# Mixing stage of a hybrid decoder trunk: both head pairs of the recurrence take its steps together, decay and key tiles first, placed by a clock

## The chip, the cores and the metric

The kernel runs on one core of one Trainium2 chip. The metric is device time in microseconds (us) of a whole execution, as the median of several runs. The profile is of one further execution, taken by the hardware profiler; TensorE is called PE in it, VectorE DVE, ScalarE ACT, GpSimd POOL and SyncE SP.

## The reference

Two layers, each a feed-forward half (SwiGLU), a mixing of tokens, and a second feed-forward half, over 512 tokens of width 1024. The change lies in the mixing, whose input projection gives 20 tiles of 128 columns: attention (8 query heads, 2 key/value heads, window 128), RWKV-7 (4 heads of 64) and a short gated convolution. Cut to what matters:

```python
def rwkv7_time_mix(p, mu, w0, w_w2, a0, a_w2, w_g2, k_k, k_a, r_k, gn_w, gn_b):
    p = p + mu * (token_shift(p) - p)
    r, k, v, wd, ad, gd = jnp.split(p, ...)
    w_log = -jax.nn.softplus(-(w0 + jnp.tanh(wd) @ w_w2)) - 0.5
    decay = jnp.exp(-jnp.exp(w_log))
    a = jax.nn.sigmoid(a0 + ad @ a_w2)
    g = jax.nn.sigmoid(gd) @ w_g2
    kk = (k * k_k) / norm over each head
    k = k * (1.0 + (a - 1.0) * k_a)
    def step(S, inp):                       # one token; S is 64x64 a head
        s_kk = S @ kk_t
        S = S * w_t - s_kk (kk_t * a_t) + v_t k_t
        return S, S @ r_t
    ...
    y = groupnorm(y) * gn_w + gn_b          # mean and variance of each head
    return (y + sum(r * k * r_k) * v) * g
```

## The kernel before

Everything is kept transposed: features on the 128 partitions, the 512 tokens along the row. The large projections are done in three products each (mm3, L117 to L123), on values split into a high part and a remainder: L121 high weights by high input, L122 high weights by the remainder, L123 the weights' remainder by the high input. Weights arrive whole (wraw, two buffers); ScalarE casts them to wH (L133) and VectorE subtracts to get wL (L135), four buffers each. A tile of 128 output columns is 8 x 3 products of 128x512, in PSUM under the tag "mm" (two banks). The recurrence of each head pair has a PSUM tag of its own (r0, r1), attention uses "x", two banks each.

The recurrence is worked in chunks of 64 tokens. A head pair q (two heads, 128 partitions) goes through rwkv(q), in this order, with PE's steps by the names that the trace shows:

- ps_w and ps_a (L753, L755): decay and rate from the low-rank tile lo. ps_kk: the norms of the keys. VectorE: cumulative products P of the decay (16 scans for both pairs, L771), their reciprocal iP (L779), the reciprocal norm rn (L780), kk, k and the scaled tiles.
- ps_bo: the bonus. ps_c (L811): two sets of chunk products, B and K.
- An inverse of each chunk's triangular matrix: 16x16 blocks go by DMA to a layout of 64 partitions, are inverted there in 15 double steps on VectorE (elim, L839), and come back by DMA. Two levels of products (ps_x, ps_t, ps_tt, L897) join the blocks.
- ps_vN, ps_beN, ps_kaN, ps_ta (L853): transposes. ps_xv (L874), ps_w (L916): their products with the inverse. The result, negated, is AX/Wn (L917).
- ps_gn (L926 to L930) and ps_o (L942 to L946): each chunk's transition and output. ps_s (L954): six sequential state steps. ps_ys (L960).
- ps_m, ps_v (headsum, L610), ps_g (L980): the group norm's mean and variance, and the gate.

Each of these products is between 64x64 blocks of the two heads and two chunk parities. A block stands on rows 0 to 63 or 64 to 127 of the array by the partitions of its input, and on its columns by the partitions of its output. ps_gn and ps_o use all four combinations of halves; ps_x, ps_t, ps_tt, ps_w (L916) and ps_xv use two, since the output keeps its input's half.

Attention goes through four blocks of 128 queries: scores (ps_sc, L1001, L1003), softmax on ScalarE (exponentials, L1026) and VectorE, transposes (ps_pt, L1041) and ps_av (L1059).

The order: products() is a generator that yields after each large product; it delivers the 20 tiles (keys kt and values of attention, queries 0 to 3, then lo, k0, r0, v0, k1, r1, v1, gd, six of the convolution), and then six tiles of the output projection, which need attention. rwkv(0), rwkv(1) and attention are generators too; each yields the PE time of the step just issued. A loop gives them credit in proportion to the work left:

```python
while credit > 0 and more:
    product_step()          # one group of large products, 0.65 of credit
```

with the work of a pair set to 29.8, attention 15.2 and the products 129.6. Each engine then runs its queue in order. In shape, small tiles before the activations (gap, gap2, shift, shift2) set where the tiles lie in the memory.

Of the kernel before, what the change touches and what calls it, by code (L numbers as in the profile page):

```python
# [17 lines left out]
P = 128  # L18
# [14 lines left out]
GAP = 448  # L33
GROUPS = ((0, 12), (12, 22))
RWKV_WORK, ATT_WORK, FILL_WORK = 29.8, 15.2, 129.6


def _columns(spec):
# [14 lines left out]
    ("ident", P), ("bones", P), ("bones2", 2), ("su", CH), ("iu", CH), ("diag", CH),  # L53
# [5 lines left out]
def trunk_kernel(ctx, tc, ins, out, layers=L, phases=("ffn1", "mix", "ffn2")):  # L59
# [7 lines left out]
    shift = ctx.enter_context(tc.tile_pool(name="shift", bufs=1))  # L67
    shift.tile([P, GAP // 4], F32, name="shift")
    hnp = [ctx.enter_context(tc.tile_pool(name=n, bufs=KD)) for n in ("hnp", "hnp2")]
    shift = ctx.enter_context(tc.tile_pool(name="shift2", bufs=1))  # L70
    shift.tile([P, (512 - GAP) // 4], F32, name="shift2")
# [45 lines left out]
    def mm3(acc, w, k, x, sl, start, stop):  # L117

        wH, wL, xH, xL = w[0][:, k], w[1][:, k], weave(x[0][:, sl]), weave(x[1][:, sl])
        acc = paired(acc)  # L120
        mm(acc, wH, xH, start=start, stop=False)  # L121
        mm(acc, wH, xL, start=False, stop=False)  # L122
        mm(acc, wL, xH, start=False, stop=stop)  # L123
# [213 lines left out]
    def ffn(l, w_in, w_pair, w_out, hn, im, ss, need, then, first, ready, coming):  # L337
# [6 lines left out]
        with tc.tile_pool(name="act", bufs=1) as ap_:  # L344
            ap_.tile([P, GAP // 4], F32, name="gap", tag="gap")
            com = {n: tuple(ap_.tile([P, 4, H2], F32R, name=x, tag="com", bufs=8) for x in ("comH", "comL")) for n in ("P1", "P2", "T3", "T4")}
            ap_.tile([P, (512 - GAP) // 4], F32, name="gap2", tag="gap2")
# [235 lines left out]
    def mix(l, hn, ss, mp, then, ready):  # L583
# [42 lines left out]
        def shifted(pt, j, z):  # L626

            act(pt.like(z), pt.view, AF.Copy, scale=got["om"][:, j : j + 1])
            for b, n in enumerate((T // 2, T // 2 - 1)):
                later = z[:, b * T // 2 + 1 :][:, :n]  # L630
                stt(later, pt.view[:, b, :n], mu[:, j : j + 1], later, ALU.mult, ALU.add)
            return z

        def products():
# [10 lines left out]


# [6 lines left out]
            got.update(om=om, w0h=w0h, a0h=a0h)  # L653
            kt = A("kt")
# [6 lines left out]
            yield  # L661
            pv = psum([P, NB, P], "ps_vt")
            for b in range(NB):
                nc.tensor.transpose(pv[:, b], vr[:, b * P : (b + 1) * P], cst("ident"))
# [4 lines left out]
            rq4 = rq.rearrange("p (b i g) -> p b i g", i=4, g=2)  # L669
            for i in range(4):  # L670
# [4 lines left out]
                if i == 1:  # L675
                    pk = headsum(ksq, "ps_ks")
# [4 lines left out]
                sq = EA("qsq")  # L681
                act(pt.like(sq), pt.view, AF.Square)
                yield
                pq = psum([P, NB, 2], "ps_q")
                for b in range(NB):
                    mm(pq[:, b], sq[:, b * P : (b + 1) * P], cst("bones2"), start=True, stop=True)
                act(rq4[:, :, i], pq, AF.Sqrt, bias=vals["eps64"])
            nc.vector.reciprocal(rq, rq)
# [3 lines left out]
            got["lo"] = shifted((yield from tile_()), 6, S(1, "lo"))  # L692
            act(got["lo"][:64], got["lo"][:64], AF.Tanh)
# [51 lines left out]
        def rwkv(q):  # L745

            R = f"r{q}"
            c1 = slice(q, q + 1)
            cw = slice(q * P, (q + 1) * P)
            lo = got["lo"]  # L750

            pw = psum([P, T], "ps_w", R)
            mm(pw, lw[:64, cw], lo[:64], start=True, stop=True)  # L753
            pa = psum([P, T], "ps_a", R)
            mm(pa, lw[64:, cw], lo[64:], start=True, stop=True)  # L755
            yield 1.7
            kp = prm(l, "kk")[:, c1]
            sq = EQ(q, "kksq")
            act(sq, k_[q], AF.Square, scale=kp)
            d0 = EQ(q, "decay")  # L760
            act(d0, pw, AF.Tanh, bias=got["w0h"][:, c1], scale=0.5)
            act(d0, d0, AF.Exp, bias=vals["nhb"], scale=-HB)
            a_ = S(q, "a")
            act(a_, pa, AF.Tanh, bias=got["a0h"][:, c1], scale=0.5)
            pk = headsum(sq, "ps_kk", R)
            yield 0.9
            ts(a_, a_, 0.5, 0.5, ALU.mult, ALU.add)
            Pt = S(q, "P")
            for c in range(NC):
                cs = slice(c * CH, (c + 1) * CH)  # L770
                nc.vector.tensor_tensor_scan(Pt[:, cs], d0[:, cs], zero, 1.0, ALU.mult, ALU.add)  # L771
            pc = small(f"pc{q}", NC)
            nc.vector.tensor_copy(pc, Pt[:, CH - 1 :: CH])

            rn = EQ(q, "rn")
            ts(rn, pk, 1e-24, None, ALU.max)
            act(rn, rn, AF.Sqrt)
            iP = S(q, "iP")
            nc.vector.reciprocal(iP, Pt)  # L779
            nc.vector.reciprocal(rn, rn)  # L780
            kk = S(q, "kk")
            stt(kk, k_[q], kp, rn, ALU.mult, ALU.mult)
            t = EQ(q, "k2")
            ts(t, a_, -1.0, prm(l, "ka")[:, c1], ALU.add, ALU.mult)
            k2 = k_[q]
            stt(k2, t, 1.0, k2, ALU.add, ALU.mult)
            bo = S(q, "bonus")
            stt(bo, r_[q], prm(l, "rk")[:, c1], k2, ALU.mult, ALU.mult)
            pb = headsum(bo, "ps_bo", R)
            yield 0.9  # L790

            AR = U(q, "AR", [P, 2, NC, CH])
            tt(AR[:, 0, :, 1:], chunks(Pt)[:, :, : CH - 1], chunks(kk)[:, :, 1:], ALU.mult)
            nc.vector.tensor_copy(AR[:, 0, :, 0], chunks(kk)[:, :, 0])
            be = a_
            tt(be, kk, a_, ALU.mult)
            tt(be, be, iP, ALU.mult)
            tt(AR[:, 1], chunks(r_[q]), chunks(Pt), ALU.mult)
            ka = iP
            tt(ka, k2, iP, ALU.mult)  # L800
            tt(bo, pb, v_[q], ALU.mult)


            def pairs(src, name):
                M = U(q, name, [P, 2, NB, 2, CH])
                pts = [psum([P, NB, 2, CH], "ps_c", R) for _ in range(2)]
                for b in range(NB):
                    for c in range(2):
                        n = 2 * b + c
                        for e in range(2):  # L810
                            mm(pts[e][rows[c], b], src[rows[e], n * CH : (n + 1) * CH], AR[rows[e], :, n], start=True, stop=True)  # L811
                msk = con[:, CON["su"][0] : CON["iu"][1]].unsqueeze(1).to_broadcast([P, NB, 2 * CH])
                for e in range(2):
                    tt(M[:, e].rearrange("p b a t -> p b (a t)"), pts[e].rearrange("p b a t -> p b (a t)"), msk, ALU.mult)
                yield 1.4
                return M

            B_ = yield from pairs(be, "B")
            LT = B_[:, :, :, 0]
# [551 lines left out]
```

## Time and profile before

| | |
|---|---|
| time, median of 3 runs | 1866.52 us (1865.02 to 1866.69) |
| the profiled execution | 1866.04 us, its span 1864.0 us |
| PE busy | 1828.7 us, 98% of the span |
| VectorE busy | 1398.4 us, 75% |
| ScalarE busy | 836.3 us, 45% |
| GpSimd busy | 130.9 us, 7% |
| DMA | 308.24 MB, mean 165 GB/s |
| mixing stage, layer 1 | 372.77 to 615.56 us |
| mixing stage, layer 2 | 1286.62 to 1529.21 us |

A page of the profile tells shares of the span; a group of instructions is given as line, engine, operation, output and inputs, shape, count, then busy time and mean duration in ns, then the engine's idle time just before and what ended it. In a timeline each row is start, duration, engine, line and instruction. Matmuls overlap their successors, so a row's duration is longer than the distance to the next.

### The profile page before, as it was taken

The page shows a single profiled execution, that of the slowest core. Times are in us where ns is not written, and L with a number is a line of the kernel's source. Part 1 is how long each engine was busy: PE and PEld are TensorE (multiplying, and loading weights), DVE is VectorE, ACT ScalarE, POOL GpSimd, SP SyncE. Part 2 cuts the span into 40 slices and gives each one's busy share as a digit, 9 for nine tenths or more (in the row PEclk, how much of TensorE's full clock was granted, in tenths as well). Part 3 has the DMA queues.
Part 4 walks back from the last instruction along what each step waited for, and adds up shares of the span by engine and source line. Part 5 has one row for each costly group of instructions (what it writes and reads, how often), then busy time and mean ns, then how long its engine had stood idle before and what let it go on. Part 6 is the DMA issues. An engine that isn't in the chain of part 4 may idle for free.

```text
span 1864.0 us, 33421 instructions
## 1 busy us (share of the span) xinstructions
PE 1828.7 (98%) x13664; PEld 1644.4 (88%) x13664; DVE 1398.4 (75%) x2202; ACT 836.3 (45%) x1272; POOL 130.9 (7%) x212
## 2 busy tenths in 40 slices
PE   8999999999999999999999999999999999999999
PEld 6889899986777999899999988999767788998998
DVE  7687677867986887777878786777589778874872
ACT  4443255346422555245345524544563335532551
POOL 0101110100000000110100020110000000100100
PEclk8999999999999999999999999999999999999999
DMA  7667876621122475886737688773212125775752
GB/s 307 225 185 234 263 197 202 221 83 46 58 55 72 136 195 176 296 223 195 246 112 197 171 272 228 192 229 114 101 56 59 53 68 161 209 227 139 203 144 68
DMA packets 104313, 308.24 MB, mean 165 GB/s; under 512 B 23392, under 2 KB 24416, under 8 KB 103136
## 3 DMA queue, kind: packets, MB, share of 16 engines
q1 hardware_dynamic: 75936, 203.34, 32.3%
q0 software_dynamic: 28224, 102.77, 21.7%
q8 instruction: 107, 1.75, 0.4%
q14 instruction: 46, 0.38, 0.1%
HBM read 302.66 MB, written 3.41 MB: 164 GB/s over the span
## 4 chain that ended last, share of the span: by engine, by line
PE 71%; DVE 13%; DMA 7%; issue 4%; ACT 4%; POOL 1%; SPq 0%; POOLq 0%; DVEq 0%; ACTq 0%
PE ps_mm L121 11%; PE ps_mm L122 10%; PE ps_mm L123 10%; PE ps_d L420 6%; PE ps_d L422 6%; PE ps_d L421 6%; PE ps_f L420 3%; PE ps_f L422 3%; PE ps_f L421 3%; DMA wada<-in_wadaT 2%; DVE wL L135 2%; PE ps_g L422 2%; PE ps_g L420 2%; PE ps_g L421 2%; ACT wH L133 1%
## 5 line engine op out<-in xcount | busy, mean ns | idle before, releaser
L133 ACT CAST wH<-wraw 128x1024 fp32r<-128x1024 f32 (+2 forms) x292 | 266.1, 918 | 434.7 <-PE ps_mm L122 190.2
L135 DVE TENSOR_TENSOR wL<-wraw,wH 128x1024 fp32r<-128x1024 f32 (+2 forms) x292 | 307.2, 1058 | 105.1 <-ACT wH L133 104.4
L123 PE MATMUL ps_mm<-actH,wL 128*128 128x512 f32 (+1 forms) x784 | 281.5, 359 | 2.8 <-DVE wL L135 2.8
L121 PE MATMUL ps_mm<-actH,wH 128*128 128x512 f32 (+1 forms) x784 | 281.6, 359 | 0.0
L122 PE MATMUL ps_mm<-actL,wH 128*128 128x512 f32 (+1 forms) x784 | 281.2, 359 | 0.0
L121 PE MATMUL ps_mm<-hnH,wH 128*128 128x512 f32 (+1 forms) x760 | 267.5, 359 | 5.7 <-ACT hnH L133 2.9
L122 PE MATMUL ps_mm<-hnL,wH 128*128 128x512 f32 (+1 forms) x760 | 266.5, 353 | 0.5
L123 PE MATMUL ps_mm<-hnH,wL 128*128 128x512 f32 (+1 forms) x760 | 266.4, 353 | 0.6 <-DVE wL L135 0.6
L420 PE MATMUL ps_d<-comH,wH 128*128 128x256 f32 x816 | 224.7, 275 | 0.3 <-ACT s L446 0.3
L421 PE MATMUL ps_d<-comL,wH 128*128 128x256 f32 x816 | 224.4, 275 | 0.0
L422 PE MATMUL ps_d<-comH,wL 128*128 128x256 f32 x816 | 224.4, 275 | 0.0
L192 DVE SCALAR_TENSOR_TENSOR wada<-wada,crep 128x1024 f32<-128x1024 f32 x140 | 167.7, 1219 | 48.8 <-DMA wada<-in_wadaT 48.2
L135 DVE TENSOR_TENSOR wL<-sum,wH 128x1024 fp32r<-128x1024 f32 x102 | 124.9, 1224 | 71.5 <-ACT wH L133 71.3
L123 PEld LDWEIGHTS ps_mm<-actH,wL 128*128 128x128 f32 x784 | 149.1, 190 | 20.3 <-DVE wL L135 3.6
L121 PEld LDWEIGHTS ps_mm<-hnH,wH 128*128 128x128 f32 x760 | 143.4, 191 | 24.9 <-issue 3.8
L121 PEld LDWEIGHTS ps_mm<-actH,wH 128*128 128x128 f32 x784 | 149.1, 190 | 16.8
L122 PEld LDWEIGHTS ps_mm<-actL,wH 128*128 128x128 f32 x784 | 149.0, 190 | 16.8
L123 PEld LDWEIGHTS ps_mm<-hnH,wL 128*128 128x128 f32 x760 | 145.5, 191 | 19.3 <-issue 4.3
L122 PEld LDWEIGHTS ps_mm<-hnL,wH 128*128 128x128 f32 x760 | 145.4, 192 | 17.2 <-DVE hnL L277 1.6
L420 PEld LDWEIGHTS ps_d<-comH,wH 128*128 128x128 f32 x816 | 156.7, 192 | 0.9 <-ACT s L446 0.9
L422 PEld LDWEIGHTS ps_d<-comH,wL 128*128 128x128 f32 x816 | 156.7, 192 | 0.0
L421 PEld LDWEIGHTS ps_d<-comL,wH 128*128 128x128 f32 x816 | 156.7, 192 | 0.0
(354 smaller groups left out, 3855.6 us busy)
## 6 DMA issues: line engine op xcount, KB each, us to landing
wada<-in_wadaT POOLq DMA_DIRECT2D x128, 512.0 KB, 4.8
wraw<-in_wmi SPq DMA_DIRECT2D x40, 512.0 KB
wraw<-in_w2p SPq DMA_DIRECT2D x36, 512.0 KB
wraw<-in_w1p SPq DMA_DIRECT2D x32, 512.0 KB
wraw<-in_w1o SPq DMA_DIRECT2D x32, 384.0 KB
wraw<-in_w2o SPq DMA_DIRECT2D x32, 384.0 KB
wraw<-in_w1i SPq DMA_DIRECT2D x20, 512.0 KB
wraw<-in_w1o SPq DMA_DIRECT2D x32, 320.0 KB
```

What stands on the lines that cost most here:

```text
L121: mm(acc, wH, xH, start=start, stop=False)
L122: mm(acc, wH, xL, start=False, stop=False)
L123: mm(acc, wL, xH, start=False, stop=stop)
L133: nc.scalar.copy(hi, src)
L135: return nc.vector.tensor_sub(lo, src, hi.bitcast(F32))
L192: stt(w, w, 1.0, crep, ALU.mult, ALU.mult, accum_out=out_)
L420: mm(acc, wH, xH, start=start and i + k == 0, stop=False, skip_group_check=True)
L421: mm(acc, wH, xL, start=False, stop=False, skip_group_check=True)
L422: mm(acc, wL, xH, start=False, stop=k == 3, skip_group_check=True)
```

## The change

- The two rwkv(q) become one rwkv(): every step does pair 0 and pair 1 (which comes first alternates).
- The projection's tiles come in the order lo, k0, k1, keys, values, queries 0 to 3, r0, r1, v0, v1, gd, convolution. The recurrence begins when k1 is done and waits inside for r and for v.
- The blocks of both pairs are inverted together on 128 partitions in one pass of 15 double steps.
- ps_xv, ps_x, ps_t, ps_tt and ps_w (now ps_w2) write to all four combinations of halves; what lands on the other half is fetched back by three copies instead of one (gathered).
- The decay and rate products are issued in halves of the row, alternating between the two row halves.
- The squares of the queries are summed by four products of 32 columns side by side (ps_q) and turned by four transposes, instead of 16 products with a width of 2 each.
- The mean of y is taken out of the values beforehand (the matrix cen in place of the identity in ps_vN), so ps_m goes.
- A generator's step yields its PE time and a latency until its next step. A clock adds 0.65 for each group of large products and the PE time for each step; the step that has been ready longest comes once the clock has reached it, otherwise large products do. A step's first matmul stands behind the latest large product in PE's order (lead).
- The pads gap and shift go; the constants grow by 608 bytes a partition.

The diff, cut:

```diff
-GAP = 448
-RWKV_WORK, ATT_WORK, FILL_WORK = 29.8, 15.2, 129.6
+STEP = 0.65
...
-    ("ident", P), ("bones", P), ("bones2", 2), ("su", CH), ("iu", CH), ("diag", CH),
+    ("ident", P), ("bones", P), ("bones2", 32), ("cen", P), ("su", CH), ("iu", CH), ("diag", CH),
...
+        def pe(*args, **kw):
+            m = mm(*args, **kw)
+            if lead[0] is not None:
+                tc.add_manual_dep(m.ins, lead[0].ins.name, ORDER, reason="a step stands behind the large products before it")
+                lead[0] = None
+            return m
...
+            got["lo"] = shifted(pt, 6, S(1, "lo"))
+            act(got["lo"][:64], got["lo"][:64], AF.Tanh)
+            for q in range(2):
+                k_[q] = shifted((yield from tile_()), 2 + q, S(q, "k"))
+            done.add("rwkv")
...
-                pq = psum([P, NB, 2], "ps_q")
-                for b in range(NB):
-                    mm(pq[:, b], sq[:, b * P : (b + 1) * P], cst("bones2"), start=True, stop=True)
-                act(rq4[:, :, i], pq, AF.Sqrt, bias=vals["eps64"])
+            pq = psum([P, T], "ps_q")
+            for i in (3, 2, 1, 0):
+                pe(pq[32 * i : 32 * i + 32], cst("bones2"), sqs[i], start=True, stop=True)
+            root = sqs[0]
+            act(root, pq, AF.Sqrt, bias=vals["eps64"])
...
             for q in range(2):
-                k_[q] = shifted((yield from tile_()), 2 + q, S(q, "k"))
                 r_[q] = shifted((yield from tile_()), 0 + q, S(q, "r"))
+            done.add("r")
+            for q in range(2):
                 v_[q] = shifted((yield from tile_()), 4 + q, S(q, "v"))
-                done.add(f"rwkv{q}")
+            done.add("v")
...
-        def rwkv(q):
+        def rwkv():
...
+            for q in range(2):
+                act(sq[q], k_[q], AF.Square, scale=kp[q])
+            yield 0, 3.0
+            pw, pa = banks("ps_w"), banks("ps_a")
+            for sl in HALVES:
+                for q in range(2):
+                    for e, pt in enumerate((pw, pa)):
+                        pe(pt[q][:, sl], lw[rows[e], cw[q]], lo[rows[e], sl], start=sl is HALVES[0], stop=sl is HALVES[1])
+            pk = sums(sq, "ps_kk", (0, 1), ("x", "x"))
...
+            for q in range(2):
+                Pt[q], iP[q], kk[q], pc[q] = S(q, "P"), S(q, "iP"), S(q, "kk"), small(f"pc{q}", NC)
+                for c in range(NC):
+                    cs = slice(c * CH, (c + 1) * CH)
+                    nc.vector.tensor_tensor_scan(Pt[q][:, cs], d0[q][:, cs], zero, 1.0, ALU.mult, ALU.add)
+                nc.vector.tensor_copy(pc[q], Pt[q][:, CH - 1 :: CH])
+                nc.vector.reciprocal(iP[q], Pt[q])
+                nc.vector.reciprocal(rn[q], rn[q])
+                stt(kk[q], k_[q], kp[q], rn[q], ALU.mult, ALU.mult)
+                ts(a_[q], a_[q], 0.5, 0.5, ALU.mult, ALU.add)
+                t = EQ(q, "k2")
+                ts(t, a_[q], -1.0, kap[q], ALU.add, ALU.mult)
+                stt(k_[q], t, 1.0, k_[q], ALU.add, ALU.mult)
+            be, ka = a_, iP
+            AR = [U(q, "AR", [P, 2, NC, CH]) for q in range(2)]
+            for q in range(2):
+                tt(be[q], kk[q], a_[q], ALU.mult)
+                tt(be[q], be[q], iP[q], ALU.mult)
+                tt(ka[q], k_[q], iP[q], ALU.mult)
+                tt(AR[q][:, 0, :, 1:], chunks(Pt[q])[:, :, : CH - 1], chunks(kk[q])[:, :, 1:], ALU.mult)
+                nc.vector.tensor_copy(AR[q][:, 0, :, 0], chunks(kk[q])[:, :, 0])
+            yield 3.2, 8.0
+            while "r" not in done:
+                yield 0, STEP
...
+            corners = [(b, e, c) for b in range(NB) for e, c in ((1, 1), (1, 0), (0, 1), (0, 0))]
+            def quarters(name, n=1, w=CH):
+                return [[psum([P, n, NB, w], name, R[q]) for _ in range(2)] for q in range(2)]
+            def gathered(pts, j):
+                return [(slice(0, P), 0, pts[0][:, j])] + [(rows[c], 1, pts[1][rows[1 - c], j]) for c in range(2)]
...
+            def each(q, pts, j, lhs, rhs):
+                for b, e, c in corners:
+                    pe(pts[q][e][rows[c ^ e], j, b], lhs[q][rows[c], e, b], rhs[q][rows[c], e, b], start=True, stop=True)
...
+        clock, more, stuck = 0.0, True, False
         while more or live:
             for n in [n for n in waiting if n in done]:
-                live[n] = waiting.pop(n)()
...
+                live[n], ready_[n] = waiting.pop(n)(), clock
+            n = min(live, key=ready_.get, default=None)
+            if n and (ready_[n] <= clock or stuck or not more):
+                clock = max(clock, ready_[n])
+                lead[0] = latest["large"]
+                step = next(live[n], None)
...
+                    clock += step[0]
+                    ready_[n] = clock + step[1]
+                stuck = False
+            else:
+                step = next(prod, "end")
+                more, stuck = step != "end", step == "stuck"
+                clock += STEP * (step is None)
```

More of the change, by code (lines that the diff above doesn't have):

```diff
@@ new lines, in rwkv @@
+            qs = both()
+            pt = [psum([P, NC, CH], "ps_ys", R[q]) for q in range(2)]
+            for q in qs:
+                for c in range(1, NC):
+                    for e in range(2):
+                        pe(pt[q][rows[e], c], St[q][rows[e], c], RT[q][rows[e], c], start=True, stop=True)
+            for q in qs:
+                tt(chunks(y[q])[:, 1:], chunks(y[q])[:, 1:], pt[q][:, 1:], ALU.add)
+            sq = [EQ(q, "gnsq") for q in range(2)]
+            for q in qs:
+                act(sq[q], y[q], AF.Square)
@@ L985, in attention @@
+            yield 3.6, 0.0
         def attention():
@@ L1097, in mix @@
+            if LOG:
+                print(f"{clock:.1f}", n, ready_.get(n), step)
         xr = []
```

496 lines of the change are left out of this document (245 added, 251 removed).

## The prediction, made before the changed kernel was run

> **What bounds the kernel now.** I read the page first, then windows around the two mixing stages, then groups and the timeline inside the first.
>
> ```profile
> PE 1828.7 (98%) x13664; PEld 1644.4 (88%) x13664; DVE 1398.4 (75%) x2202; ACT 836.3 (45%) x1272; POOL 130.9 (7%) x212
> 372.77:615.56 242.79, 238.16 (x2109) 187.03 (x2108) 183.07 (x390) 105.91 (x220) 1.79 (x6) 1.00 0.20 62
> 1286.62:1529.21 242.59, 238.00 (x2108) 186.89 (x2108) 183.02 (x390) 105.82 (x220) 1.81 (x6) 1.00 0.21 62
> ```
>
> TensorE (PE) is busy 98% of the span, so what the change takes from PE's program is worth time, and every idle stretch it opens costs its full length. The diff touches little beside the two mixing stages (the windows; columns: length, then busy time of PE, weight loads, VectorE, ScalarE and GpSimd, the granted clock, the DMA share, GB/s). There PE idles 242.79 - 238.16 = 4.63 us. VectorE is busy 183.07 of 242.79, a share of 75%: it has slack on average, but not in every stretch. DMA (share 0.20) and GpSimd are far from a bound.
>
> How a stage's PE time divides is seen in its timeline, at a switch from the large projection products to a step of the recurrence and back (columns: start, busy, engine, line, instruction, how many).
>
> ```profile
> 551.61 0.38 PE L123 MATMUL ps_mm<-hnH,wL 128*128 128x512 f32 x1
> 551.83 0.38 PE L121 MATMUL ps_mm<-hnH,wH 128*128 128x512 f32 x1
> 552.14 1.15 PE L897 MATMUL ps_x<-T,B 64*64 64x64 f32 x32
> 553.22 0.48 PE L122 MATMUL ps_mm<-hnL,wH 128*128 128x512 f32 x1
> 553.53 0.38 PE L123 MATMUL ps_mm<-hnH,wL 128*128 128x512 f32 x1
> 361.78 0.28 PE L121 MATMUL ps_mm<-actH,wH 128*128 128x256 f32 x1
> 361.89 0.28 PE L122 MATMUL ps_mm<-actL,wH 128*128 128x256 f32 x1
> ```
>
> Large products follow each other every 0.22 us (551.61, 551.83), half ones every 0.11. The code has 552 full and 240 half ones per stage: 552 x 0.2157 + 240 x 0.1115 = 145.8 us (mean pitches of such runs), untouched by the change. The other 97.0 us are small steps and the switches. A switch costs: 551.83 to 552.14 is 0.31 instead of 0.22, and 553.22 to 553.53 again, so 0.19 or more per visit. Over all 60 visits of a layer, the starts of which I summed, it is 0.29 (17.7 us beyond the instructions' own pitch).
>
> **What the change saves on PE**, per layer, from rows of before.
>
> ```profile
> L926 PE MATMUL ps_gn<-beN,AX x32: 218/218/267, 565.3 to 566.5; 64*64 64x64 f32 x32
> L930 PE MATMUL ps_gn<-AX,beN x32: 218/218/218, 565.6 to 566.7; 64*64 64x64 f32 x32
> 559.22 1.09 PE L916 MATMUL ps_w<-AX,TT 64*64 64x128 f32 x16
> 560.24 0.48 PE L122 MATMUL ps_mm<-y5L,wH 128*128 128x512 f32 x1
> 545.96 1.02 PE L610 MATMUL ps_v<-gnsq,con 128*128 128x512 f32 x2
> 546.82 1.02 PE L980 MATMUL ps_g<-gd,gw 128*128 128x512 f32 x2
> L686 PE MATMUL ps_q<-con,qsq 128*128 128x2 f32 x32 | 4.2, 254 | 0.0
> ```
>
> - *Four quadrants.* ps_x fills two quadrants of the array: 32 in 1.08 us, 34 ns each. ps_gn already fills four: its three groups of 32 start within 565.3 to 566.7, 96 in 1.5 us, 16 ns each. The change puts ps_x, ps_t, ps_tt (320 per layer, two passes counted as two) and ps_xv (64) into four: 384 x 18 ns = 6.9. ps_w's 64 at (560.24 - 559.22)/16 = 64 ns go to half: 2.0. Together 8.9. If quadrants in this pattern did not overlap, nothing.
> - *Query norms.* 32 passes busy 4.2 become 8 passes of four column groups and 4 transposes. A 512-wide pass takes 0.43 (546.82 - 545.96, two passes). Eight are 3.4 if they run one by one, 0.9 if the column groups overlap; I take overlap, as ps_gn's quadrants do, and 0.8 for transposes and their extra visit: saving 2.5, bounds 0 and 3.
> - *Decay and rate products* (ps_w, ps_a, 64 rows each): now issued alternately on both row halves, 3.4 to 1.7: 1.7, bound 0. *The mean of y* (ps_m) goes: 4 x 0.43 = 1.7.
> - *Visits.* In the order in which the two programs are built, a layer has 60 stretches of small work before and 41 after: 19 at 0.19 to 0.29, 5.0.
>
> Sum 19.8, say **20 us per layer**. VectorE also loses one of two 15-step inversions, no term of mine since PE did not wait for it.
>
> Two edits I cost at nothing, by these groups:
>
> ```profile
> L420 PE MATMUL ps_d<-comH,wH 128*128 128x256 f32 x816 | 224.7, 275 | 0.3 <-ACT s L446 0.3
> L121 PE MATMUL ps_mm<-actH,wH 128*128 128x256 f32 x34 | 9.5, 280 | 0.0
> L133 ACT CAST wH<-wraw 128x1024 fp32r<-128x1024 f32 x21 | 21.8, 1041 | 17.7 <-PE ps_mm L122 11.5 <-DMA wraw<-in_wmi 6.1
> ```
>
> The removed pads and the larger constants move every later tile in the memory. com and act lie differently to each other before, and products from them take the same 275 and 280, so place shows no price; it would reach both feed-forward stages if it did. The inverse's transfers on SP's queue are 35 instead of 36 per layer, but 16 or 17 stand in a row where 8 did, ahead of weight loads. ScalarE's casts waited 6.1 us for weights and none of it reached PE; if it did after, up to 6 per layer, which I keep in the upper end only.
>
> **What it costs: waits that PE did not have.** The order on VectorE decides. Before, a weight split (wL, L135) lies amid the decay work:
>
> ```profile
> 447.39 1.56 DVE L771 TENSOR_TENSOR_SCAN P<-decay,zero 128x64 f32<-128x64 f32 x8
> 448.87 1.20 DVE L135 TENSOR_TENSOR wL<-wraw,wH 128x1024 fp32r<-128x1024 f32 x1
> 450.66 3.34 DVE L779 RECIPROCAL iP<-P 128x512 f32<-128x512 f32 x1
> 453.92 0.70 DVE L1008 COPY_PREDICATED Sc<-con,ps_sc 128x256 f32<-128x256 int32 x2
> L782 DVE SCALAR_TENSOR_TENSOR kk<-k,par,rn 128x512 f32<-128x512 f32 x2 | 1.5, 740 | 0.0
> L797 DVE TENSOR_TENSOR a<-a,iP 128x512 f32<-128x512 f32 x2 | 1.4, 678 | 0.0
> L784 DVE TENSOR_SCALAR k<-a,par 128x512 f32<-128x512 f32 x2 | 0.9, 474 | 0.0
> L761 ACT ACTIVATE decay<-ps_w,w0h 128x512 f32<-128x512 f32 x2 | 1.4, 678 | 0.0
> L762 ACT ACTIVATE decay<-decay,v_nhb 128x512 f32<-128x512 f32 x2 | 1.4, 722 | 0.1
> ```
>
> After, both pairs' decay work is queued as one block. As built, no split lies among 16 scans at 1.56/8 = 0.19 (3.1), five reciprocals (iP and rn of both pairs, rk of the keys) at 453.92 - 450.66 = 3.26 (16.3), nineteen passes over 128x512 (4 at 0.474, 3 at 0.74, 12 at 0.678, each less the 0.08 by which the first reciprocal overlaps its successor: 10.7) and four small ones (0.3): **30.4 us**. The split behind the block is that of the eighth tile, the third of the queries, and in PE's order the 81st large product behind the decay step reads it: 81 x 0.2157 = 17.5, and 1.5 for the transposes of v and the key norm. The block begins about 2.4 after the step's last product (tanh, exp, and the other pair's tanh, 0.68 + 0.72 + 0.68, and their latency). So the split is ready 2.4 + 30.4 + 1.2 = 34.0 after the step and PE wants it at 19.0: **a stall of 15 us** per layer. It is 10 if the block's first part runs while the step's products still do and the passes overlap more, 18 if the passes over both pairs also wait for ScalarE. What queues behind the block are all later splits, and behind those the weight transfers, since two raw buffers are all there are.
>
> A long gap has a second price (windows, then PE's rows with the wait in brackets):
>
> ```profile
> 215.00:220.00 5.00, 2.56 (x12) 1.92 (x12) 3.80 (x7) 1.04 (x1) 0.00 (x0) 1.00 0.66 238
> 220.00:224.30 4.30, 4.30 (x14) 3.48 (x13) 3.75 (x5) 0.44 (x1) 1.62 (x2) 0.60 0.93 285
> 219.59 0.48 PE L123 MATMUL ps_mm<-actH,wL 128*128 128x512 f32 x1 [2.44 <-DVE wL L135]
> 221.59 0.63 PE L121 MATMUL ps_mm<-actH,wH 128*128 128x512 f32 x1
> 222.01 0.63 PE L122 MATMUL ps_mm<-actL,wH 128*128 128x512 f32 x1
> ```
>
> After a wait of 2.44 us in the first feed-forward the granted clock falls from 1.00 to 0.60 in the mean of the next 4.3 us, and products go 0.42 apart (221.59, 222.01) instead of 0.22. A share of 0.40 of 4.3 us is 1.7 lost. I book 1.7 once per layer, for the long stall, bounds 0 and 3.4 (two stalls). The Trainium skill, "TensorE: Matmul & The Clock Gate", "What's actually happening", speaks against this change here: it states that the clock halves after at least one idle window of about 3.4 us and comes back after about 3.4 us of work. By it the price would be an estimated 1.7 us for each stall long enough to fill a window; the trace agrees on the length, but shows the fall after a profile gap of only 2.44.
>
> **Two more waits.** The rows are ScalarE's in the first block of attention, PE's beside them, then groups.
>
> ```profile
> 419.21 1.28 ACT L1026 ACT_TABLE_LOAD   x1 [4.78 <-DVE mx L1020]
> 424.53 0.67 ACT L628 ACTIVATE lo<-ps_mm,om 128x512 f32<-128x512 f32 x1
> 425.23 0.38 PE L123 MATMUL ps_mm<-hnH,wL 128*128 128x512 f32 x1
> 426.65 0.52 PE L1041 MATMUL ps_pt<-con,Sc 128*128 128x128 f32 x3 [1.05 <-DVE Sc L1029]
> L1026 ACT ACTIVATE Sc<-Sc,mx,rq 128x128 f32<-128x128 f32 x32 | 15.3, 481 | 3.9 <-DVE mx L1020 3.8
> L917 ACT ACTIVATE AX<-ps_w 128x512 f32<-128x512 f32 x4 | 2.4, 598 | 4.4 <-PE ps_w L916 4.4
> ```
>
> A tile that leaves PSUM behind the softmax's eight exponentials waits: ScalarE idled 4.78 for the row maxima and spent 424.53 - 419.21 = 5.32 on them before it took up the tile lo; PE showed 1.05 of waiting at 425.23 to 426.65. After the change the tile there is the first r, and nothing of the recurrence can run yet (its next step waits for both r tiles), so PE has only 30 large products, 6.5 us, against 4.78 + 5.32 = 10.1: **3.6 us**, bounds 0 (the exponentials lie elsewhere) and 5. Second, when the convolution's tiles are out, the last attention block is not: the products stop and PE's order has 208 small ones in one stretch. The negated Wn copies (4 x 0.598 = 2.4) stand on ScalarE behind the last block's eight exponentials (5.3), and PE has 12 large products ahead (2.6): 5.3 + 2.4 - 2.6 = **5.1**, bounds 2 and 10. The rest of what each step waits for is covered by large products as before, and I leave the 4.63 of idle time as it is; if that cover is gone, each of some ten steps would show the 0.5 to 1 us that ps_pt showed.
>
> **Sum per layer:** -20 + 15 + 1.7 + 3.6 + 5.1 = +5.4 us; for two layers +10.8. The profiled execution took 1866.04 us, 2.04 around its span of 1864.0, and lies 0.48 under the median 1866.52; 1866.52 + 10.8 = **1877**.
>
> **Rivals.**
> - *A: all waits bite*, as above: 1877; with their bounds (waits 18 to 33 per layer against a saving of 18 to 20) 1862 to 1892.
> - *B: faster, since only VectorE's block bites.* The two waits on ScalarE disappear if softmax and r tile fall apart by a few microseconds in the real timing, which a 15 us stall ahead of them may do (queues catch up while PE stands). Then -20 + 11 to 15 + 1.7 gives -3 to -7 per layer, 1852 to 1860, middle 1855. The point from which it decides: waits of 20 us per layer. For it: PE waited only 1.05 at the like place before. Against: the order on ScalarE is fixed.
> - *C: nothing new bites*, and all 20 are gained: 1866.5 - 40 = 1827. It needs VectorE's block to take under 16 us; the rows of its reciprocals alone, 16.3, speak against.
> - *D: quadrants and column groups do not overlap* in these patterns, so that the change does not do what it says: 8.9 + 2.5 of the saving go, and -8.6 + 25.4 gives +16.8 per layer, 1900. ps_gn's rows speak against it.
>
> **How the numbers follow.** A 0.56, B 0.26, C 0.07, D 0.11. A measurement of this kernel can tell 0.2%, 3.7 us, from no change. Of A about 0.49 lies above 1870.2, 0.06 within, 0.01 below; of B 0.22 below and 0.04 within. So faster 0.30, same 0.10, slower 0.60. The range: C is left out (0.07), and half of D (0.06) with the far end of B: 1845 to 1898. A alone: 1862 to 1892.
>
> **What would show it.** Right: in the profile after, VectorE full for 30 us from the first scan, and a PE wait of 10 us or more on a split (wL) in the query tiles, with a granted clock under 1 behind it; ps_x, ps_t, ps_w2 at 16 to 32 ns each; waits at the r tiles and at ps_pt or ps_gn behind the last convolution tile. Wrong: PE idle in the stage under 20 us (then the kernel is faster), or pitches of the quadrant steps still at 34 ns (then D).

## The result and the profile after

The changed kernel takes 1888.04 us (median of 5 runs, 1881.36 to 1889.61) against 1866.52 before: the ratio is 1.0099, 95% interval 1.008 to 1.0119, by which it is slower by 0.0099 x 1866.5 = 18.5 us (the two medians lie 21.5 apart). The profiled execution took 1889.61 us, its span is 1887.6.

The page after, its first line, and the windows of the two mixing stages. So that kernels with another order can be compared, each stage here runs from the 2195th (7607th) large product of the trace to the 3005th (8417th), which are the same products in every kernel. The first fence is the kernel before in these bounds, the others are the changed kernel; the columns are those of the windows in the prediction.

```profile
378.33:625.61 247.28, 242.48 (x2140) 190.99 (x2139) 187.06 (x397) 109.00 (x227) 0.85 (x4) 1.00 0.21 66
1278.20:1521.75 243.55, 239.29 (x2122) 188.40 (x2121) 181.11 (x386) 106.67 (x220) 1.85 (x6) 1.00 0.20 60
```

```profile
PE 1800.8 (95%) x13648; PEld 1632.1 (86%) x13648; DVE 1401.7 (74%) x2190; ACT 837.6 (44%) x1278; POOL 130.2 (7%) x208
```

```profile
376.97:634.66 257.69, 229.66 (x2133) 185.71 (x2131) 188.47 (x391) 109.96 (x230) 0.59 (x2) 0.94 0.21 64
1292.96:1544.39 251.43, 223.72 (x2115) 181.38 (x2113) 185.17 (x383) 108.44 (x224) 1.58 (x4) 0.95 0.20 60
```

PE is busy 12.8 us less in the first stage (242.48 to 229.66) and 15.6 less in the second, though its granted clock there is only 0.94 and 0.95 in the mean. The stages are longer all the same, by 10.4 and 7.9 us: together 18.3, which is the difference that the ratio gives. (The feed-forward halves between the two stages took 648 to 658 us in the profiled executions of all the kernels below, in no order that follows the edits; the 23.6 us between the two profiled executions hold 5.7 of that.)

Where PE's idle time lies in the first stage is told by its chain of waits (PE's instruction, the instruction waited for, us in total, times, the longest):

```profile
PE ps_mm L119 <- DVE wL L131: 9.6, 1, 9.6
PE ps_mm L117 <- DVE r L627: 3.2, 1, 3.2
PE ps_gn L634 <- ACT AX L990: 2.8, 2, 1.9
PE ps_mm L117 <- DVE lo L627: 2.7, 1, 2.7
PE ps_mm L117 <- ACT yrH L129: 2.1, 1, 2.1
PE ps_pt L634 <- DVE Sc L1112: 2.0, 1, 2.0
PE ps_sc L634 <- DVE Sc L1090: 1.9, 1, 1.9
PE ps_mm L117 <- ACT hnH L272: 1.3, 1, 1.3
PE ps_mm L117 <- ACT qsq L706: 1.3, 1, 1.3
```

The longest one is the split behind VectorE's decay block. VectorE's timeline, with the block's first and last instructions:

```profile
400.84 0.43 DVE L828 TENSOR_SCALAR a<-a 128x512 f32<-128x512 f32 x1 [2.81 <-ACT a L814]
401.45 0.66 DVE L823 TENSOR_TENSOR_SCAN P<-decay,zero 128x64 f32<-128x64 f32 x3 [0.18 <-ACT decay L813]
...
404.37 3.35 DVE L825 RECIPROCAL iP<-P 128x512 f32<-128x512 f32 x1
...
426.47 3.35 DVE L702 RECIPROCAL rk<-rk 128x512 f32<-128x512 f32 x1
...
430.94 2.35 DVE L131 TENSOR_TENSOR wL<-wraw,wH 128x1024 fp32r<-128x1024 f32 x2
...
507.52 0.69 DVE L954 TENSOR_TENSOR T<-C,con 128x512 f32<-128x512 f32 x1 [2.86 <-DMA C<-di]
508.13 0.77 DVE L1090 COPY_PREDICATED Sc<-con,ps_sc 128x256 f32<-128x256 int32 x2
```

From 400.84 to 430.94 VectorE does nothing but the block, 30.1 us, and only then takes the two splits that are due. PE reached the first at 422.56 and stood until 432.21. Around that wait, and around a much shorter one at the first tile, PE's timeline and the windows behind them show the clock:

```profile
392.21 0.45 PE L117 MATMUL ps_mm<-hnH,wH 128*128 128x512 f32 x1 [2.74 <-DVE lo L627]
392.50 0.38 PE L118 MATMUL ps_mm<-hnL,wH 128*128 128x512 f32 x1
...
393.57 0.63 PE L119 MATMUL ps_mm<-hnH,wL 128*128 128x512 f32 x1
393.99 0.63 PE L117 MATMUL ps_mm<-hnH,wH 128*128 128x512 f32 x1
```

```profile
432.50:437.50 5.00, 5.00 (x13) 3.87 (x13) 1.16 (x2) 1.05 (x1) 0.00 (x0) 0.50 0.60 211
393.10:396.60 3.50, 3.50 (x10) 2.75 (x10) 2.16 (x5) 3.49 (x5) 0.00 (x0) 0.51 0.34 105
```

Behind the wait of 9.65 us eleven products go 0.42 apart instead of 0.22 (granted clock 0.50), behind that of 2.74 us eight. With two later spells it is 30 such products in the first stage, 30 x 0.21 = 6.3 us; in the second stage it is 17, 3.6 us. Small steps run at half clock too and are not in this count: PE is busy with ps_gn for 5.26 us in the first stage, 3.56 before. The kernel before has no half clock in its mixing stages.

### The profile page after: what moved, and what is told of

It is laid out like the page before. It is cut to its first block, busy times and chain, and to the rows that moved or that the text cites. A ratio compares the mean times of both kernels' runs of the same rounds, so it can differ in the third digit from the quotient of the medians.

```text
span 1887.6 us, 33343 instructions
## 1 busy us (share of the span) xinstructions
PE 1800.8 (95%) x13648; PEld 1632.1 (86%) x13648; DVE 1401.7 (74%) x2190; ACT 837.6 (44%) x1278; POOL 130.2 (7%) x208
## 5 line engine op out<-in xcount | busy, mean ns | idle before, releaser
L117 PEld LDWEIGHTS ps_mm<-hnH,wH 128*128 128x128 f32 x760 | 144.9, 193 | 51.2 <-issue 10.9
```

## The experiments

Each kernel is timed beside the kernel before on its own chip; "stages" is the sum of both mixing stages in the bounds above, from the one profiled execution of each kernel (that of kernel 8 was the fastest of its four runs, that of kernel 6 the slowest of its five). For the kernel before it is 490.8, for the changed kernel 509.1. Differences between kernels that are smaller than their intervals are not told apart by these runs.

| kernel | median us | ratio to before | 95% interval | stages us |
|---|---|---|---|---|
| the change | 1888.04 | 1.0099 | 1.0080 to 1.0119 | 509.1 |
| 1 block spread | 1852.53 | 0.9916 | 0.9888 to 0.9944 | 480.8 |
| 2 halves again | 1885.87 | 1.0103 | 1.0080 to 1.0126 | 505.8 |
| 3 before, with quadrants | 1885.07 | 1.0098 | 1.0073 to 1.0123 | 506.1 |
| 4 before, with all savings | 1877.65 | 1.0051 | 1.0030 to 1.0073 | 500.7 |
| 5 spread, halves | 1854.74 | 0.9930 | 0.9908 to 0.9953 | 478.4 |
| 6 spread, exponentials apart | 1855.43 | 0.9939 | 0.9917 to 0.9961 | 480.9 |
| 7 spread, key tile first | 1850.31 | 0.9910 | 0.9882 to 0.9938 | 476.6 |
| 8 combination | 1845.96 | 0.9879 | 0.9854 to 0.9903 | 470.6 |
| 9 combination, halves | 1856.73 | 0.9934 | 0.9910 to 0.9958 | 479.5 |
| 10 same, attention sooner | 1847.28 | 0.9888 | 0.9866 to 0.9909 | 468.7 |
| 11 combination, attention sooner | 1849.07 | 0.9905 | 0.9888 to 0.9922 | 474.1 |

### 1. VectorE's block spread

```diff
                 nc.vector.reciprocal(iP[q], Pt[q])
+                yield 3.2 * (1 - q), 6.0
                 nc.vector.reciprocal(rn[q], rn[q])
...
                 stt(k_[q], t, 1.0, k_[q], ALU.add, ALU.mult)
+                yield 0, 6.0
...
                 nc.vector.tensor_copy(AR[q][:, 0, :, 0], chunks(kk[q])[:, :, 0])
-            yield 3.2, 8.0
+                yield 0, 4.0
```

> The changed kernel, but with VectorE's decay block of both pairs cut into six parts (each pair's scans with iP, then rn with kk and k, then be, ka and AR), with 4 to 6 us of large products let in between, so that weight splits get in. Theory (VectorE's queue makes the stall at the query tiles): the waits of 9.65 and 1.26 us and the half-clock products behind them (11 x 0.21 = 2.3) go in both layers, 2 x 13.2 = 26 us; 1888 becomes about 1862, VectorE's work unchanged. Rival (the weights themselves come late, since only two raw buffers are held, or the joint steps as such starve PE): the wait moves to a later tile and the time stays within 5 us of 1888.

Measured 1852.53, stages 28.3 us shorter (257.7 to 243.6, 251.4 to 237.2). VectorE's timeline of this kernel has the splits inside the block, and its waits no longer name a split of 9.6:

```profile
407.32 3.30 DVE L827 RECIPROCAL rn<-rn 128x512 f32<-128x512 f32 x1
...
413.40 1.20 DVE L131 TENSOR_TENSOR wL<-wraw,wH 128x1024 fp32r<-128x1024 f32 x1
...
422.39 1.22 DVE L131 TENSOR_TENSOR wL<-wraw,wH 128x1024 fp32r<-128x1024 f32 x1
```

```profile
PE ps_gn L634 <- ACT AX L992: 2.8, 2, 1.9
PE ps_mm L117 <- DVE lo L627: 2.7, 1, 2.7
...
PE ps_mm L119 <- DVE wL L131: 1.8, 1, 1.8
```

The theory stands: late weights, as in the rival, would have kept or moved the wait, but the longest one on a split is now 1.8, so the order of VectorE's queue made the stall, and one block of 30 us is the difference between a kernel that is 1% slower than before and one that is 0.8% faster. The time fell by more than the 26 us expected, 0.0183 x 1866.5 = 34 us by the two ratios: the wait for the first r tile (3.2) went as well, unasked, and the part beyond the stages' 28.3 lies in the feed-forward halves (658 to 652 us in the two profiled executions), which the edit does not touch. Of the 28.3, 22.5 are waits (PE idle 55.7 to 33.3 us in both stages) and 5.8 PE's busy time, mostly half clock that went with them.

### 2, 5. Two halves instead of four quadrants

```diff
-    return [(slice(0, P), 0, pts[0][:, j])] + [(rows[c], 1, pts[1][rows[1 - c], j]) for c in range(2)]
+    return [(slice(0, P), e, pts[e][:, j]) for e in range(2)]
...
-    pe(pts[q][e][rows[c ^ e], j, b], lhs[q][rows[c], e, b], rhs[q][rows[c], e, b], start=True, stop=True)
+    pe(pts[q][e][rows[c], j, b], lhs[q][rows[c], e, b], rhs[q][rows[c], e, b], start=True, stop=True)
```

(and likewise ps_xv and ps_w2), once in the changed kernel, once in the spread one.

> The changed kernel with ps_xv, ps_x, ps_t, ps_tt and ps_w2 back on two halves of the array (one bank for each head, two copies out instead of three). Theory (the saving of the four quadrants is real and lies on PE's path): 384 x 18 ns + 2.0 = 8.9 us a layer come back, 1888 + 18 = 1906; ps_x at 34 ns again. Rival (the pace of these steps is set by the copies behind them, or PE waits there anyway): within 4 us of 1888.

> The kernel with the spread block (1852.5) with ps_xv, ps_x, ps_t, ps_tt and ps_w2 back on two halves. In the changed kernel itself that cost nothing. Theory 1 (what the quadrants save on PE is given back as waiting for the chain of copies behind each step, whatever stands before): within 4 us of 1852.5, with 7 us a layer more in the steps and about 6 less in PE's waits. Theory 2 (only the stalls of the changed kernel hid it; with the long block gone PE is the bound and 7.4 us a layer come back): about 1867.

Neither lost time beyond the noise: 1885.87 beside 1888.04, 1854.74 beside 1852.53, with overlapping intervals; the stages of the profiled executions are even 3.3 and 2.4 us shorter. Yet PE's own work did grow: from start to start, waits left out, ps_x, ps_t (with ps_tt), ps_xv and ps_w (ps_w2 and the decay product together) took 8.35 us in the first stage of the changed kernel and 15.6 with halves, 14.5 us more in the two stages. Kernel 2's windows of the two stages tell what made up for it:

```profile
378.69:636.29 257.60, 231.68 (x2132) 189.70 (x2131) 183.20 (x381) 107.46 (x226) 0.59 (x2) 0.97 0.21 64
1294.54:1542.74 248.20, 225.96 (x2115) 185.31 (x2113) 178.85 (x373) 105.40 (x219) 1.58 (x4) 0.98 0.20 61
```

PE idles 7.6 us less in both stages together (28.0 and 27.7 in the changed kernel, 25.9 and 22.2 here). And its busy time is only 4.2 us longer instead of 14.5, since less of it runs at half clock: the granted clock is 0.97 and 0.98 here, 0.94 and 0.95 in the changed kernel. So about half of what the quadrants saved came back as waiting, and the other half and a little more as half clock. In the halves' waits, the items at the end of attention and of the inverse are smaller than in the changed kernel (ps_gn and ps_pt had 2.8 and 2.0, ps_sc 1.9):

```profile
PE ps_o L634 <- issue: 2.2, 1, 2.2
...
PE ps_gn L634 <- issue: 0.9, 1, 0.9
...
PE ps_sc L634 <- DVE Sc L1090: 0.7, 1, 0.7
PE ps_gn L634 <- ACT AX L990: 0.6, 1, 0.6
```

In time, the rival of kernel 2 and theory 1 of kernel 5 hold; but the waits of kernel 5 fell by 3.5 and 5.5 us a layer instead of 6, and the clock, which neither text names, did the rest.

### 3, 4. The savings without the joint steps

Into the kernel before go the quadrants alone (3), then also the query norms in column groups, the alternating decay products and the centred values, with the pads out (4). Pair by pair, with the old order and credit:

```diff
-            tt(X, px, rep2(f"lev{lev}", NB), ALU.mult)
+            for r, e, x in gathered(px):
+                tt(X[r, e], x, rep(f"lev{lev}", NB)[r], ALU.mult)
```

> The kernel before, with only the four quadrants for ps_xv, ps_x, ps_t, ps_tt and ps_w (pair by pair, old tile order, old credit). Theory: 8.9 us a layer saved on PE, no new block on VectorE: 1866.5 - 18 = 1849. Rival (the saving needs the joint steps, since a pair alone waits for its copies between levels): 1862 to 1867.

> The kernel before with all of the change's savings on PE that need no joint steps: four quadrants, query norms by four column groups, decay and rate products alternating, values centred so that ps_m goes, pads out; old tile order, pair by pair, old credit. Theory: 8.9 + 2.5 + 1.7 + 1.7 = 14.8 us a layer, 1866.5 - 30 = 1837, since before has none of the three new waits. Rival (old order can't use it: ps_q's step opens a wait of its own, or the credit now places steps too early): 1850 or more.

Both are slower than before, by 1.0 and 0.5%; both theories were wrong, since neither allowed for a loss, and so was kernel 3's rival. (Kernel 4's rival, 1850 or more, has no upper end.) The groups and the waits of kernel 3 tell why; the first line is the kernel before:

```profile
L902 DVE TENSOR_TENSOR X<-ps_x,con 128x512 f32<-128x512 f32 x4 | 2.7, 683 | 1.1 <-PE ps_x L897 1.1
```

```profile
L908 DVE TENSOR_TENSOR X<-ps_x,con 64x256 f32<-64x256 f32 x8 | 3.4, 421 | 0.8 <-PE ps_xv L880 0.7
...
L917 DVE TENSOR_TENSOR TT<-TT,ps_tt 128x256 f32<-128x256 f32 x4 | 1.7, 421 | 0.6 <-PE ps_tt L902 0.5
```

```profile
PE ps_tt L902 <- DVE T L913: 2.8, 3, 1.5
PE ps_o L949 <- DVE N L940: 2.3, 1, 2.3
...
PE ps_x L902 <- DVE TT L917: 1.4, 2, 0.9
```

```profile
555.08 0.68 PE L902 MATMUL ps_tt<-TT,X 64*64 64x64 f32 x16 [0.80 <-DVE T L913]
557.30 1.12 PE L902 MATMUL ps_tt<-TT,X 64*64 64x64 f32 x16 [1.54 <-DVE T L913]
556.83 0.42 DVE L913 TENSOR_TENSOR T<-T,ps_t 64x256 f32<-64x256 f32 x1
```

A copy of 64 partitions takes as long as one of 128 (0.42 us at 256 columns), so the three pieces that fetch a quadrant step back cost VectorE 1.26 us where one piece of 128x512 took 0.68. There is a second cost in the edit: each step now fills both PSUM banks of its pair's tag, where it filled one. ps_tt reads X and TT, and yet it waits for T: its second half starts at 557.30, when the last piece has come out of the bank that ps_t had filled (556.83 + 0.42). The wait of ps_x for TT is of the same kind, so 4.2 us of kernel 3's waits are for banks and not for data. PE's waits rose from 4.8 to 12.3 in the first stage. Its busy time did not fall (242.80 us, before 242.48), though the five steps took 14.6 instead of 18.6: with a granted clock of 0.98, half clock took that back. Kernel 4 did save on PE, 8.3 us of busy time in both stages, and its idle time there rose from 9.1 to 27.2. How much is due to the copies and how much to the banks no run separates.

### 6, 7, 8. The other waits

Kernel 6 issues the exponentials two at a time. Kernel 7 takes the attention's keys as the first tile and issues the first pair's norm and gate before the second's. Kernel 8 has both, and the step that needs the inverse 3 us later:

```diff
                 for i in range(4):
+                    if i % 2 == 0:
+                        yield 0.53 * (g == 0 and i == 0), 1.3
                     act(Sc[:, i], Sc[:, i], AF.Exp, ...)
...
-    order = [rw(j) for j in (6, 2, 3)] + [np.r_[512:768], pairs] + ...
+    order = [np.r_[512:640]] + [rw(j) for j in (6, 2, 3)] + [np.r_[640:768], pairs] + ...
...
-            yield 1.4, 16.0
+            yield 1.4, 19.0
```

> The spread kernel, with the softmax's exponentials issued two at a time, 1.3 us of large products apart, instead of eight in a row. Theory (ScalarE's row of exponentials holds up what queues behind it): the waits at ps_pt, ps_gn behind the last convolution tile (2.01 + 1.94 + 0.85) halve, 2.4 a layer and a clock window less now and then: 1846. Rival (the last block's scores come late, so that any order of the exponentials ends at the same time): 1850 to 1855.

> The spread kernel with two more edits: the attention's key tile goes first (it leaves PSUM by a single copy), then lo, k0, k1; and at the end the first pair's norm and gate are issued before the second's instead of interleaved with them. Theory (each 2 to 3 us wait also costs a half-clock window): the waits of 2.74 and 2.12 go, with windows of 8 and 7 products at 0.21: 8 us a layer, 1837. Rival (decay step a tile later, the chain of the recurrence ends later by as much): 1848 to 1855.

> All of it: block spread, exponentials two at a time, key tile first, first pair's end ahead of the second's, and the step that needs the inverse 3 us later, so that scores are not queued behind its DMA on VectorE (waits of 1.18 and 1.56). Theory: 1852.5 - 5 - 16 - 3 = 1829, PE idle in the first mixing stage under 8 us. Rival (the recurrence's chain sets the stage's end: what is taken away early comes back at the last step): 1845 to 1853.

Kernel 6 bought nothing: the waits at ps_pt and ps_gn went from 5.4 to 0.9, and new ones at ps_o (2.5), ps_x (1.8) and an output tile (2.7) took their place. Its time lies at the end of its rival's range; the rival's reason, late scores, was not tested. Kernel 7 won a quarter of what was expected in the stages (4.2 us of 16), and by the ratio 1 us, within the noise: the wait at the first tile fell from 2.74 to 0.84, but a wait of 2.2 for a transpose is new, and that for yrH stayed at 2.1, because VectorE's order still alternates between the two pairs there (its two reciprocals, 6.57 us, come before either pair's next step). The combination has the lowest median, 1.2% under before, 17 us above what was expected and in its rival's range; PE idles 13.9 us in its first stage, where under 8 was expected. Its waits lie at the end of the recurrence's and attention's chains:

```profile
PE ps_mm L117 <- DVE h L324: 2.5, 1, 2.5
PE ps_gn L634 <- ACT AX L991: 2.1, 1, 2.1
PE ps_o L634 <- DVE N L1009: 2.0, 1, 2.0
PE ps_t L634 <- DVE X L970: 1.8, 1, 1.8
```

### 9, 10, 11. Combination with halves, attention sooner

Kernel 9 is 8 with halves; 10 is 9 with attention's steps 1.3 us sooner after the scores and 1.1 instead of 1.3 us between exponentials; 11 is the same on 8.

> The combination (1846) with ps_xv, ps_x, ps_t, ps_tt and ps_w2 back on two halves. Theory 1 (the chain behind the steps, with three copies out of PSUM for each quadrant step instead of two, takes back what PE saves): 1842 to 1849, no slower than the combination. Theory 2 (with most waits gone PE is the bound at last and the quadrants pay): 1858 to 1861.

> The same, with the attention's steps placed 1.3 us sooner after the scores and 1.1 instead of 1.3 us between pairs of exponentials, so that its last block ends about 6 us of clock sooner and the products do not run out ahead of it. Theory (the last attention block ends the products' stretch): the waits at ps_gn, ps_o and at the first y4 product (2.11, 2.03, 2.52 in the combination) shrink by half, 3 us a layer, 6 below the kernel beside it. Rival (steps placed ahead of their data only move the wait into ps_pt): within 2 us of it.

> The combination with the quadrants (1846), and with attention's steps placed sooner as in the run before. Theory (the two gains add: sooner attention took 10.8 us off both mixing stages with halves, the quadrants 8.9 in the combination): both stages together 460 us, time about 1837 or a ratio to the kernel before of 0.983. Rival (with the quadrants PE arrives sooner at the same late data, so one gain hides the other): stages 466 to 470, a ratio of 0.987 to 0.990.

In the combination the quadrants are worth 8.9 us in the stages (470.6 against 479.5) and 10 us by the ratios: near theory 2, at 60% of the 14.5 us of PE work in two layers. Sooner attention takes 10.8 us from 9 to 10, but not by its theory, which wanted the waits to shrink: PE's idle time in both stages fell by only 1.4 us, and its busy time by 9.4, since no half clock is left in kernel 10's stages (second stage of 9, then of 10):

```profile
1271.54:1510.54 239.00, 229.56 (x2115) 188.16 (x2113) 179.41 (x371) 105.51 (x219) 1.59 (x4) 0.97 0.22 63
1274.10:1505.57 231.47, 223.23 (x2114) 183.28 (x2113) 178.76 (x371) 105.22 (x219) 1.58 (x4) 1.00 0.22 65
```

The two gains do not add: with both (11) the ratio is 0.9905, not 0.983, and the stages take 474.1. What PE no longer spends in quadrants it waits for, at ps_pt above all, and the half clock is back (0.97 in the first stage):

```profile
PE ps_pt L634 <- DVE Sc L1115: 2.9, 1, 2.9
...
PE ps_t L634 <- DVE X L970: 1.5, 1, 1.5
```

The quadrants were tried in four pairs of kernels. The table gives the kernel with halves less the one with quadrants (a positive number is a gain by the quadrants), in us over both stages of the profiled executions, and by the ratios of the whole time:

| halves less quadrants | stages | PE busy | PE idle | by the ratios |
|---|---|---|---|---|
| 2 less the change | -3.3 | +4.2 | -7.6 | +0.7 |
| 5 less 1 | -2.4 | +6.6 | -9.0 | +2.6 |
| 9 less 8 | +8.9 | +15.4 | -6.5 | +10.3 |
| 10 less 11 | -5.4 | +4.6 | -10.1 | -3.2 |

The halves' extra work on PE is 14.5 us in every pair, and 6.5 to 10.1 of it always comes back as less waiting. What turns the sign is the half clock, which makes the difference between 14.5 and the column of PE's busy time. The mean clock over all runs of each kernel goes the same way: 0.981 with quadrants and 0.985 with halves, 0.990 and 0.993, 0.992 and 0.991, 0.991 and 0.994. Only the third pair's times are clear of the noise. Kernels 8 and 10 are level.

## Why the prediction was right or wrong

The forecast was 1877, slower; measured was 1888, in the range and on the side of case A, with a gain of PE time as booked and waits as booked, each off in size. That the total came this close is partly luck: the stall was booked 4 us a layer too high, the clock and the waits left out too low. The range stated for A is also narrower than its terms allow: their own bounds add up to waits of 12 to 36 us a layer, not 18 to 33, and 33 against a saving of 18 gives 1896, not 1892.

- **The saving of 20 us** was right as PE time: busy time fell by 12.8 in the first stage with 6.3 us of half-clock products in it, 19.1. Of its terms, ps_x is now 2.18 us for 128 (17 ns each, forecast 16), the norms' ps_q went from 3.72 to 1.00 with 0.56 for the transposes (2.2, forecast 2.5), and the visits from 63 to 44. The quadrants gave 7.3, forecast 8.9. One saving was in no term: PE was busy with ps_c (128 products) for 8.58 us before and for 3.96 after. The change takes it for both pairs at once and with the two heads in the other order; which of these did it was not tested. Part of the agreement with 20 is therefore luck: this saving and the small steps' half clock, which the 19.1 leaves out, roughly offset each other.
- **That a microsecond off PE is a microsecond of the stage** is the step that failed, and it failed silently: the sum took the saving in full and the waits beside it, when a part of PE's saved time only reappears as waiting, and as half clock behind the waits. Kernels 2 and 5 show that for the quadrants' 14.5 us in two layers: 7.6 and 9.0 came back as waiting, the rest and a little more as half clock. The page's 98% for PE was true of its time and said nothing of the next 2%: the steps' distance from their data had presumably been laid out for the slower steps. I had also booked nothing for the three pieces instead of one (gathered), 1.26 against 0.68 us on VectorE, nor for the second PSUM bank that each step takes (kernel 3).
- **VectorE's block** was 30.1 us, forecast 30.4. The stall was 9.6 and 1.3 us, forecast 15: the mis-sized term is the 2.4 us between the step's last product and the block. In the trace the block begins at 400.84 and the first large product behind the step starts only at 401.30: ScalarE's tanh and exp ran beside the step's ps_kk. That is 2.9 of the 4 us; PE also took 20.0 us to get there instead of 19.0. It was the lower bound, 10, and the 9.65 stays just under the 10 us or more that was named as the sign.
- **The clock** was booked at 1.7 a layer and took 6.3 and 3.6: not only the long wait, but also those of 2.74, 1.92 and 2.12 us brought half-clock spells. With the small steps it is more (ps_gn alone 1.7 a layer).
- **The two waits on ScalarE** were 3.2 at the r tile (forecast 3.6), and 2.0 + 2.8 at ps_pt and ps_gn (4.8, forecast 5.1).
- **What I left out**: 2.7 at the first tile (lo, whose four shifted sums on VectorE stood behind a split), 2.1 at yrH, and 1.9 at ps_sc. The last is a transfer that I had costed at nothing: the blocks of the inverse land late, VectorE waits 2.86 us for them at its head (L954, row above), and the copies of the scores are queued behind. Before, the stage's 4.8 of idle time was spread over small waits; of these few are left.

By layer the forecast -20 + 15 + 1.7 + 3.6 + 5.1 reads, for the first stage, -19.1 + 10.9 + 6.3 + 3.2 + 4.8 + 6.7 for what I left out, and -2.4 net for the small waits of before against those that stayed: +10.4 measured, +5.4 forecast. (The small steps' half clock lies in the -19.1.)

Rival B (only the block bites, 1855) was not it. Rival C's 1827 would have needed all waits covered, which no kernel here reached. D fell: the quadrants overlap, though in the changed kernel that made no measurable difference to the time.

## What to carry to other kernels

When steps are grouped, look at the other engines' queues for the longest stretch that holds no work for the busiest engine, and set it against what is buffered there: here 30 us on VectorE against four buffered weight tiles, visible in the instruction order before any run, and worth 28 us of both stages once cut in six. A saving on a busy engine counts only where the steps behind it also come sooner; take it away and put it back in two different schedules before believing in it. Count the PSUM banks too: a step that takes two where it took one makes the next step wait for the copies out. And price any wait over about 2 us on PE at up to 2 us more for the clock; in the four pairs above it is the half clock that turned the sign.

## What the hardware showed unexpectedly

Over the profiled executions of the thirteen kernels, without their first 100 us, PE stood for 1.9 to 3.3 us 74 times. Behind 46 of them the granted clock was halved within 3.4 us; of 171 waits between 0.9 and 1.9 us, behind 29; all four waits over 9 us had it. The same wait, 2.74 us for lo, brought half clock in one layer of the changed kernel and none in the other.

The records of the granted clock show which wait is hit. In each execution all spells of half clock begin a whole number of steps of 3.413 us apart and last one to four such steps: in the first stage of the changed kernel they begin at 393.14, 423.86, 509.19, 553.57 and 597.94, which is 9, 34, 47 and 60 steps after the first. Cut into these steps, the thirteen executions have 57 steps at full clock in which PE idled for more than 1.90 us, and half clock followed all 57. Of 19 with 1.70 to 1.90 us it followed 6, of 6533 with less 11 (seven of these hold small steps such as ps_sc and ps_gn; why they count as idle is open). The wait for lo shows it: in the first layer it lies within one step, in the second a boundary divides it (step, PE busy, granted clock, DMA):

```profile
389.73:393.14 3.41, 0.93 (x4) 1.00 0.61 205
1318.16:1321.57 3.41, 1.76 (x16) 1.00 0.46 154
1321.57:1324.98 3.41, 2.31 (x11) 1.00 0.56 154
```

The Trainium skill, "TensorE: Matmul & The Clock Gate", "What's actually happening", states that the cold clock follows an idle window of about 3.4 us. The length agrees with the steps here; the measurement is the stricter rule, since 1.90 us of idle time in a step was enough. Its length for the way back, about 3.4 us of work, agrees too (393.15 to 396.55 in the first stage).

Where the steps fall against the program differs between the thirteen executions, so the same schedule can be hit more or less often. That would fit the spread between runs of one kernel (twelve runs of kernel 9 go from 1847.9 us at a mean clock of 0.994 to 1873.3 at 0.984), but no run set the phase, so it is not shown to be the cause.
